# Ten products of a constant block first on TensorE, x in three loads, two first weight pieces of four tiles, and the first norm's squares behind all splits of x

## The chip, the cores and the metric

The kernel runs on one core of a Trainium2 chip. The metric is device time in microseconds (us). Work is spread over TensorE (PE for products, PEld for its weight loads), VectorE (DVE), ScalarE (ACT), GpSimd (POOL) and SyncE (SP, which only issues transfers here).

## The reference, cut to what matters

A two-layer hybrid block is followed by one layer of a second block, all on a sequence of 256 positions and a width of 1024. Of the first block, only its start bears on this change:

```python
def rmsnorm(x, g):
    y = x * rsqrt(mean(x * x, axis=-1, keepdims=True) + EPS)
    return y * g
def swiglu(x, wg, wu, wd):
    return (silu(x @ wg) * (x @ wu)) @ wd        # 1024 -> 2816 -> 1024
h = x
for i in range(2):
    h = h + 0.5 * swiglu(rmsnorm(h, ffn1_norm[i]), ffn1_wg[i], ffn1_wu[i], ffn1_wd[i])
    h = h + hybrid_mixer(rmsnorm(h, mix_norm[i]), ...)
    h = h + 0.5 * swiglu(rmsnorm(h, ffn2_norm[i]), ...)
    h = h + sigmoid(rmsnorm(h, ple_norm[i]) @ ple_w_gate[i]) * (p[i] @ ple_w_proj[i])
# then the second block: pooled and convolved branches, gates, a squared-ReLU feed-forward layer
```

## The kernel before

Everything is kept channels-first: x is eight blocks of 128 channels by 256 positions (`h`). The weights are 4948 tiles of 128x128 numbers, in the order in which they are used, and come as *pieces* of up to eight tiles. A piece lands in `raw` (or, for the first six, in `extra`, which is borrowed space); ACT rounds it to `whi`, DVE takes the rest `wlo = raw - whi`, and TensorE forms each product of a tile and a block of x as three: `hs` high with `whi`, `hs` low with `whi`, `hs` high with `wlo`, each 128x256. x is split in the same way: `split_scaled` makes the high part of a block on ACT and its low part on DVE, both in `hs`, scaled by the gain in `vec`.

The first layer's products do not wait for the norm: they take x scaled by the gain alone, and the norm's factor `row` is applied when a result leaves its bank (`gate` in `ffn`). The norm is a chain: the squares of the eight blocks (`square`: ACT squares into `sq`, DVE adds into `acc`), two column sums on TensorE (`side<-ones,acc`), a few small DVE steps, two products that spread the factor over the partitions (`side<-ident,small`), and a copy to `row` on ACT. There are seven banks for results. The first four units (`heads_of`) run side by side, block of x by block of x: each block meets four tiles. From tile 32 on (tiles are counted from 0 in TensorE's order) a unit of eight tiles has a bank of its own, and tile 56 needs the first bank again, so it waits for the first `gate`.

The order in which instructions stand on each engine is made by a small event simulation (`Flow`) in the kernel's own code, with planned costs; each engine then works its instructions strictly in that order. Piece boundaries (`PIECES`) are an input to it, so a change there renames buffers and moves single instructions throughout the program. Pieces are two and four tiles, then eight each; with the two first sizes 2 and 4 all later pieces begin at 6 plus a multiple of 8. ACT's DMA queue loads 32 columns of `vec` and x in four parts (one, one, two and four blocks), SP's queue the weights.

Of the kernel before, what the change touches and what calls it, by code (L numbers as in the profile page):

```python
# [17 lines left out]
P = 128  # L18
T = 256
D = 1024  # L20
ND = D // P
# [21 lines left out]
def piece_sizes():  # L43

    out, n = [], 0
    for size in (2, 4):
        out.append(size)
    n = sum(out)
    for stop in (*WHOLE, NTILES):
        while n < stop:  # L50
            out.append(min(S, stop - n))
            n += out[-1]
    return out


PIECES = piece_sizes()
FIRST = np.concatenate([[0], np.cumsum(PIECES)])

# [135 lines left out]
class Build:  # L194
# [91 lines left out]
    def feed(self):  # L286

        self.ready = [Event() for _ in PIECES]
        self.done = [Event() for _ in PIECES]
        self.at = [None] * len(PIECES)  # L290
        for q, cnt in enumerate(PIECES):
            raw = yield from self.raws.get()
            n, w = int(FIRST[q]), cnt * P
            self.nc.sync.dma_start(raw[:, :w], self.wall[n * P * P:(n * P + w) * P].rearrange("(p w) -> p w", p=P))
            if q < 4:
                a, b = self.xpieces[q]
                self.spawn(self.x_here(a, b), self.flow.use("dma", 0.365 * (b - a)) + 2.2)
            if q == 9:
                self.nc.sync.dma_start(self.vec[:, self.early:], self.vecd[:, self.early:])
            wait = self.flow.use("dma", w * P * 4 / 360e3) + 2.35  # L300
            self.spawn(self.piece(q, raw, w), wait)
# [189 lines left out]

    def setup(self):
        nc = self.nc
        self.early = a = 32
        self.xpieces = ((0, 1), (1, 2), (2, 4), (4, 8))
        nc.scalar.dma_start(self.vec[:, :a], self.vecd[:, :a])
        for b, c in self.xpieces:
            nc.scalar.dma_start(self.h[:, b:c, :], self.xT[:, b:c, :])
        self.xev = [Event() for _ in range(ND)]
        self.flow.use("dma", 1.8)  # L500
        make_identity(nc, self.ident)
        nc.vector.memset(self.ones, 1.0)
        nc.vector.memset(self.shim, 0.0)

        nc.vector.memset(self.mask, 0.0)
        nc.gpsimd.affine_select(out=self.mask, in_=self.mask, pattern=[[1, P]], compare_op=ALU.is_ge,
                                fill=NEG, base=0, channel_multiplier=-1)
        self.chains = 0
        self.started = [Event() for _ in PIECES]
        extra = self.big.tile([P, 6, S * P], F32, name="extra", tag="X")  # L510
        self.extra = [extra[:, i, :] for i in range(6)]
        more = self.big.tile([P, 8, 8], F32, name="more", tag="more")
        self.small[18:] = [more[:, i, :] for i in range(6)]
        self.raws.free[:0] = self.extra
        for cv in self.cv.free:
            nc.vector.memset(cv[:, :16], 0.0)
        self.act(self.small[0], self.ones[:, :8], AF.Silu)

    def first(self, op, s, gain):
        for n in range(ND):  # L520
            yield self.xev[n]
            yield from self.split_scaled(op, n, self.h[:, n, :], gain(n))
            self.spawn(self.square(s, self.h[:, n, :]))

    def x_here(self, a, b):
# [907 lines left out]
```

## Time and profile before

| | |
|---|---|
| median of three runs | 1811.37 us (1809.21 to 1815.61) |
| profiled execution, its own time | 1810.08 us |
| its span in the profile | 1808.3 us |
| TensorE busy | 1778.2 us (98%) |
| VectorE busy | 1320.9 us (73%) |
| ScalarE busy | 1050.3 us (58%) |
| mean granted TensorE clock | 0.996 |

The span is the time from the first to the last instruction that the profiler recorded; 1.8 us lie around it. A row of groups gives busy time, the mean duration of one, and the idle time before the group with what ended it. A row of a timeline begins with its start and its length in microseconds, merged over equal instructions. The chain lists, in order of time, the work that the end of the program can be followed back to.

### The profile page before, as it was taken

Reading aid. Unit: us, or ns where it says so; the run is one execution under the profiler, and the core shown is the slowest. Engines: PE = TensorE matmul, PEld = TensorE weight load, DVE = VectorE, ACT = ScalarE, POOL = GpSimd, SP = SyncE. Lnnn points to the kernel's source line nnn. Section 1 sums busy time; section 2 is a strip of 40 time slices with the busy share of each in tenths; the row PEclk is TensorE's granted clock in tenths of the full one; section 3 lists DMA queues with packets and bytes.
Section 4 is the critical chain, followed back from the end, with each engine's and each line's share of the span. In section 5 each row is a group of like instructions: output and inputs, shape, how many; then the busy total and the mean of one; then the engine's idle time right before and its main releaser. Section 6 shows DMA issues by size and latency. Waiting matters only on the chain.

```text
span 1808.3 us, 36543 instructions
## 1 busy us (share of the span) xinstructions
PE 1778.2 (98%) x14904; PEld 1737.8 (96%) x14904; DVE 1320.9 (73%) x2243; ACT 1050.3 (58%) x1711; POOL 10.5 (1%) x22
## 2 busy tenths in 40 slices
PE   8999999999999999999999999999999999989997
PEld 8999999999999999999999999999999999889985
DVE  7666789888676666866678988767666689877643
ACT  6454668665455544654456866555554478656542
POOL 0000000000000000000000000000000000000000
PEclk9999999999999999999999999999999999999998
DMA  7666576665766666566667656576666653546652
GB/s 248 198 192 195 163 258 191 207 192 157 206 185 199 194 195 185 189 195 196 192 175 248 195 198 192 159 206 193 202 194 194 196 176 121 184 142 210 192 193 76
DMA packets 92552, 342.78 MB, mean 190 GB/s; under 512 B 10432, under 2 KB 10944, under 8 KB 91360
## 3 DMA queue, kind: packets, MB, share of 16 engines
q1 hardware_dynamic: 89856, 325.13, 59.3%
q0 software_dynamic: 1520, 13.73, 2.1%
q8 instruction: 116, 1.90, 0.4%
q10 hardware_dynamic: 1008, 1.59, 0.2%
q14 instruction: 52, 0.43, 0.1%
HBM read 339.26 MB, written 1.15 MB: 188 GB/s over the span
## 4 chain that ended last, share of the span: by engine, by line
PE 91%; DVE 4%; DMA 2%; ACT 2%; issue 1%; ACTq 0%; DVEq 0%; SPq 0%
PE bank L237 90%; DVE wlo L244 1%; DMA raw<-in_w 1%; PE side L237 1%; DVE cv L257 1%; ACT whi L266 0%; ACT L266 0%; PE bank L722 0%; DMA h<-in_x 0%; DVE small L257 0%; DVE hs L257 0%; DVE dec L244 0%; DVE acc L244 0%; DVE t L244 0%; DVE vv L244 0%
## 5 line engine op out<-in xcount | busy, mean ns | idle before, releaser
L237 PE MATMUL bank<-hs,whi 128*128 128x256 f32 x6928 | 1206.1, 279 | 11.7 <-ACT whi L266 7.3
L237 PEld LDWEIGHTS bank<-hs,whi 128*128 128x128 f32 x6928 | 1049.9, 189 | 18.8 <-ACT whi L266 7.6
L244 DVE TENSOR_TENSOR wlo<-raw,whi 128x1024 fp32r<-128x1024 f32 (+1 forms) x602 | 733.0, 1220 | 373.3 <-ACT whi L266 370.3
L266 ACT ACTIVATE whi<-raw 128x1024 fp32r<-128x1024 f32 (+1 forms) x602 | 635.5, 1058 | 634.3 <-issue 320.5
L237 PE MATMUL bank<-hs,wlo 128*128 128x256 f32 x3464 | 961.9, 278 | 1.9 <-DVE wlo L244 1.9
L237 PEld LDWEIGHTS bank<-hs,wlo 128*128 128x128 f32 x3464 | 653.6, 189 | 2.9 <-DVE wlo L244 2.9
L237 PE MATMUL bank<-V,whi 128*128 128x256 f32 x1920 | 326.7, 276 | 0.0
L237 PEld LDWEIGHTS bank<-V,whi 128*128 128x128 f32 x1920 | 288.8, 188 | 0.0
L237 PE MATMUL bank<-V,wlo 128*128 128x256 f32 x960 | 265.0, 276 | 0.0
L237 PEld LDWEIGHTS bank<-V,wlo 128*128 128x128 f32 x960 | 180.2, 188 | 0.0
L237 PE MATMUL bank<-whi,V 128*128 128x512 f32 x256 | 80.0, 392 | 0.0
L244 DVE TENSOR_TENSOR t<-bank,row 128x256 f32<-128x256 f32 x159 | 64.5, 416 | 14.6 <-PE bank L237 10.3
L257 DVE SCALAR_TENSOR_TENSOR cv<-bank,vec,cv 128x253 f32<-128x253 f32 (+2 forms) x144 | 63.3, 472 | 1.7 <-ACT cv L266 1.3
L244 DVE TENSOR_TENSOR vv<-bank,t 128x256 f32<-128x256 f32 x152 | 62.5, 418 | 1.9 <-ACT t L266 1.6
L244 DVE TENSOR_TENSOR V<-vv,V 128x256 fp32r<-128x256 f32 x152 | 62.2, 419 | 1.6 <-ACT V L266 1.2
L266 ACT ACTIVATE V<-vv 128x256 fp32r<-128x256 f32 x152 | 59.9, 403 | 2.1 <-DVE vv L257 1.6
L237 PEld LDWEIGHTS bank<-whi,V 128*128 128x128 f32 x256 | 48.1, 188 | 10.1
L244 DVE TENSOR_TENSOR acc<-acc,sq 128x256 f32<-128x256 f32 x108 | 45.4, 420 | 8.5 <-ACT sq L266 7.9
L237 PE MATMUL bank<-wlo,V 128*128 128x512 f32 x128 | 50.2, 392 | 0.0
L266 ACT ACT_TABLE_LOAD x37 | 47.5, 1283 | 3.7 <-issue 3.1
L266 ACT ACTIVATE dec<-dec,tb 128x256 f32<-128x256 f32 (+1 forms) x128 | 49.5, 444 | 0.1
L237 PE MATMUL bank<-x,raw 128*128 128x256 f32 x208 | 45.2, 379 | 0.0
(149 smaller groups left out, 1108.0 us busy)
## 6 DMA issues: line engine op xcount, KB each, us to landing
raw<-in_w SPq DMA_DIRECT2D x613, 512.0 KB, 4.2
dec<-cum_d POOLq DMA_DIRECT2D x8, 1536.0 KB, 10.0
extra<-in_w SPq DMA_DIRECT2D x4, 512.0 KB, 8.0
h<-in_x ACTq DMA_DIRECT2D x1, 512.0 KB, 8.3
praw<-in_p POOLq DMA_DIRECT2D x2, 256.0 KB, 3.7
gain<-in_row POOLq DMA_DIRECT2D x1, 512.0 KB, 4.2
out<-o SPq DMA_DIRECT2D x2, 256.0 KB, 2.5
out<-o ACTq DMA_DIRECT2D x2, 256.0 KB, 2.5
```

Source lines behind the costliest of these rows:

```text
L237: self.nc.tensor.matmul(ps, w, x, start=start, stop=stop, **k)
L244: self.nc.vector.tensor_tensor(out, a, b, op=op)
L257: self.nc.vector.scalar_tensor_tensor(out, a, s, b, op0=op0, op1=op1)
L266: self.nc.scalar.activation(out=out, in_=a, func=func, **k)
```

## The change

Four edits, all at the start of the program. (1) Ten products of the constant block `ones` with itself (128x128, f32, into the `side` bank) stand first on TensorE; nothing reads their result. (2) x comes in three parts (two, two and four blocks), and the first 32 columns of `vec` come through SP's queue, behind the first weight piece. (3) The first two pieces hold four tiles each, so that all later pieces begin at a multiple of 8; the piece of two tiles that stood ahead of the stretch of whole tiles (`WHOLE`) is gone, and there is one piece fewer. (4) In the first norm, the squares are started after all eight splits instead of one after each.

```diff
-    for size in (2, 4):
+    for size in (4, 4):
...
             self.nc.sync.dma_start(raw[:, :w], self.wall[n * P * P:(n * P + w) * P].rearrange("(p w) -> p w", p=P))
-            if q < 4:
+            if q == 0:
+                self.nc.sync.dma_start(self.vec[:, :self.early], self.vecd[:, :self.early])
+            if q < len(self.xpieces):
...
-        self.early = a = 32
-        self.xpieces = ((0, 1), (1, 2), (2, 4), (4, 8))
-        nc.scalar.dma_start(self.vec[:, :a], self.vecd[:, :a])
+        self.early = 32
+        self.xpieces = ((0, 2), (2, 4), (4, 8))
         for b, c in self.xpieces:
             nc.scalar.dma_start(self.h[:, b:c, :], self.xT[:, b:c, :])
...
+        for _ in range(10):
+            self.mm(self.side.free[0][:, :P], self.ones, self.ones, cost=0.4)
...
         for n in range(ND):
             yield self.xev[n]
             yield from self.split_scaled(op, n, self.h[:, n, :], gain(n))
+        for n in range(ND):
             self.spawn(self.square(s, self.h[:, n, :]))
```

What stands on ACT from the first split of x on. Before (`hs<-h,vec` is the split of a block of x, `whi<-extra` that of a weight piece, `sq` and `acc` are squares):

```order
L266 ACTIVATE hs_94<-h,vec 128x256
L266 ACTIVATE whi_78<-extra 128x256
L266 ACTIVATE hs_94<-h,vec 128x256
L266 ACTIVATE acc_111<-h 128x256
L266 ACTIVATE whi_80<-extra 128x512
L266 ACTIVATE sq_109<-h 128x256
L266 ACTIVATE hs_94<-h,vec 128x256
L266 ACTIVATE whi_82<-extra 128x1024
```

The third weight piece (`whi_82`) stands behind the split of the third block of x.

On ACT at the same place now:

```order
L266 ACTIVATE hs_94<-h,vec 128x256
L266 ACTIVATE whi_78<-extra 128x512
L266 ACTIVATE hs_94<-h,vec 128x256
L266 ACTIVATE whi_80<-extra 128x512
L266 ACTIVATE hs_94<-h,vec 128x256 x3
L266 ACTIVATE whi_82<-extra 128x1024
L266 ACTIVATE hs_94<-h,vec 128x256
L266 ACTIVATE whi_84<-extra 128x1024
```

The squares are gone from here, and the third weight piece stands behind the split of the fifth block, which comes with the last part of x.

On TensorE before, the column sums of the first norm stood in the first unit that has a bank of its own (`bank_70`), behind 34 tiles:

```order
L237 MATMUL bank_69<-hs_94,wlo_79 128x256
L237 MATMUL bank_70<-hs_94,whi_78 128x256 x2
L237 MATMUL bank_70<-hs_94,wlo_79 128x256
L237 MATMUL bank_70<-hs_94,whi_78 128x256 x2
L237 MATMUL bank_70<-hs_94,wlo_79 128x256
L237 MATMUL side<-ones,acc_111 128x128 x2
```

They stand in the midst of that unit, two of its tiles ahead of them. On TensorE now, they stand in the unit after it (`bank_71`), behind 45 tiles:

```order
L237 MATMUL bank_71<-hs_94,whi_80 128x256 x2
L237 MATMUL bank_71<-hs_94,wlo_81 128x256
L237 MATMUL bank_71<-hs_94,whi_80 128x256 x2
L237 MATMUL bank_71<-hs_94,wlo_81 128x256
L237 MATMUL side<-ones,acc_111 128x128 x2
```

They moved back by eleven tiles. The two products that spread the factor (`side<-ident,small`) moved likewise from behind 43 tiles to behind 55, one tile ahead of tile 56.

## The prediction

> **What bounds the kernel now.** I read the page first, then TensorE's waits, then the chain and the timelines of the first 31 us, where the change lies. The page:
>
> ```profile
> span 1808.3 us, 36543 instructions
> PE 1778.2 (98%) x14904; PEld 1737.8 (96%) x14904; DVE 1320.9 (73%) x2243; ACT 1050.3 (58%) x1711; POOL 10.5 (1%) x22
> ...
> PE 91%; DVE 4%; DMA 2%; ACT 2%; issue 1%; ACTq 0%; DVEq 0%; SPq 0%
> ```
>
> TensorE has work in 98% of the span, so only an idle or slow TensorE is time to win. Its waits (total, times, longest) and its pace in a long quiet window (length, PE busy with the number of products, clock, DMA share, GB/s):
>
> ```profile
> PE bank L237 <- ACT whi L266: 7.3, 2, 6.1
> ...
> 30.00:240.00 210.00, 210.00 (x1855) 1.00 0.66 194
> ```
>
> The largest wait, 7.3 us, is for the first weights, at the start. Elsewhere a product takes 210/1855 = 0.113 us, a tile of three 0.34. The chain and TensorE's timeline at the start:
>
> ```profile
> 1.66 6.04 DMA h<-in_x
> 7.72 0.51 ACT hs L266
> ...
> 8.54 0.53 ACT whi L266
> ...
> 9.11 13.64 PE bank L237 x96
> 22.75 0.44 PE side L237 x4
> ```
>
> ```profile
> 6.13 0.80 PE L237 MATMUL bank<-hs,whi 128*128 128x256 f32 x2 [6.13 <-ACT whi L266]
> ...
> 9.11 0.80 PE L237 MATMUL bank<-hs,whi 128*128 128x256 f32 x2 [1.20 <-ACT whi L266]
> ...
> 13.42 0.63 PE L237 MATMUL bank<-hs,whi 128*128 128x256 f32 x2
> ...
> 14.05 0.41 PE L237 MATMUL bank<-hs,whi 128*128 128x256 f32 x2
> ...
> 31.09 0.39 PE L237 MATMUL bank<-hs,whi 128*128 128x256 f32 x2
> ```
>
> Tile 0 starts at 6.13, tile 2 at 9.11, after a wait for the second block of x. From 9.11 TensorE does not stop, but until 14.05 a tile takes 0.63, afterwards 0.34: half rate for 4.94 us of unbroken work, then full rate. Tile 9 starts at 14.05, tile 56 at 31.09. Had tile 0 begun at full rate at 6.13 and never stopped, tile 9 would start at 9.19, so the start holds at most 4.9 us. That is 0.27% of the time; 0.3% (5.4 us) is about what a measurement of this kernel can tell from no change.
>
> **The loads.** Issue rows (SP's first six merged, SP's third and fifth, ACT's last), and issue to landing for single transfers, read in windows that hold one issue of each queue:
>
> ```profile
> 0.74 4.78 SPq L294 DMA_DIRECT2D extra<-in_w  x6
> ...
> 1.65 0.42 SPq L294 DMA_DIRECT2D extra<-in_w  x1
> ...
> 3.46 0.58 SPq L294 DMA_DIRECT2D extra<-in_w  x1
> ...
> 2.62 0.45 ACTq L498 DMA_DIRECT2D h<-in_x  x1
> ```
>
> ```profile
> extra<-in_w SPq DMA_DIRECT2D x1, 256.0 KB, 3.8
> h<-in_x ACTq DMA_DIRECT2D x1, 128.0 KB, 4.0
> ...
> extra<-in_w SPq DMA_DIRECT2D x1, 512.0 KB, 5.9
> ...
> h<-in_x ACTq DMA_DIRECT2D x1, 512.0 KB, 8.3
> ...
> extra<-in_w SPq DMA_DIRECT2D x1, 512.0 KB, 8.5
> ```
>
> The last part of x (512 KB) was issued at 2.62 and landed at 10.9. Now it is ACT's third transfer, not its fifth, and issued near 1.7. Upper bound: issued before it were 1424 KB, now 1040 KB; the 384 KB less, at the 416 GB/s of the window 9.11:14.05 (below), are 0.95 us, so 9.96. Lower bound: the third weight piece (512 KB) landed at 1.65 + 5.9 = 7.55 when it was the last of 1040 KB issued; the last part of x is now the last of 1552 KB: 7.55 + 1.26 = 8.8; rows of x twice as long may hasten the early transfers, which I allow 0.8 for, so 8.0. I take **9.0**, nearest the weight row, because both are early in the same two queues. The first part of x and the first weights, 256 KB each, land by 0.74 + 3.8 to 4.0, about 4.7. That `vec` goes by SP costs one issue (0.45 us) on SP's queue ahead of the second piece, which is wanted only after tile 3.
>
> **ACT, DVE and TensorE after it.** The durations, from the timelines of ACT, then DVE, then PE:
>
> ```profile
> 8.44 0.61 ACT L266 ACTIVATE whi<-extra 128x512 fp32r<-128x512 f32 x1
> ...
> 9.27 0.49 ACT L266 ACTIVATE hs<-h,vec 128x256 fp32r<-128x256 f32 x1
> 9.67 1.04 ACT L266 ACTIVATE whi<-extra 128x1024 fp32r<-128x1024 f32 x1
> ```
>
> ```profile
> 0.84 0.17 DVE L502 MEMSET ones<- 128x128 f32 x1 [0.84 <-PEq L1428]
> ...
> 13.34 1.22 DVE L244 TENSOR_TENSOR wlo<-extra,whi 128x1024 fp32r<-128x1024 f32 x1
> 14.48 0.48 DVE L257 SCALAR_TENSOR_TENSOR hs<-h,vec,hs 128x256 fp32r<-128x256 f32 x1
> 14.88 0.42 DVE L244 TENSOR_TENSOR acc<-acc,sq 128x256 f32<-128x256 f32 x1
> 15.21 1.22 DVE L244 TENSOR_TENSOR wlo<-extra,whi 128x1024 fp32r<-128x1024 f32 x1
> ...
> 23.23 0.16 DVE L262 TENSOR_SCALAR small<-side 128x2 f32<-128x2 f32 x1 [0.46 <-PE side L237]
> ...
> 27.28 0.42 DVE L244 TENSOR_TENSOR t<-bank,row 128x256 f32<-128x256 f32 x1 [1.87 <-ACT row L266]
> ```
>
> ```profile
> 26.21 0.61 PE L237 MATMUL side<-ident,small 128*128 128x128 f32 x4
> ```
>
> From start to start a wide `wlo` takes 1.14 us, a low split of x 0.40, an addition 0.33.
>
> *Tiles 0 to 7.* First split at 4.7, first weights 0.40 later, 0.61 long: tile 0 at 5.75 instead of 6.13. Both first pieces feed all four banks, so eight tiles follow without x's last part.
>
> *The ten products.* Two of this shape cost 0.44 us at full rate (the row `side` at 22.75), so 0.44 each at half rate: 4.4 us from 1.1, when `ones` is set, to 5.5. They lie in idle time; with 0.25 us of cover, and if the cover were gone the wait below would hide it. They begin unbroken work at 1.1, so by the 4.94 us above full rate is there near 6.0. At full rate tiles 0 to 7 are over by about 9.3 (bounded by the second piece's splits); at half rate they would end at 11.1, and tile 9 would start 0.6 later than worked out next.
>
> *Tile 8: what is late next.* On ACT the third piece now stands behind the split of block 4, which waits for x's last part at 9.0, and everything behind it waits too. Weights: 9.0 + 0.40 + 1.04 = 10.44. `wlo` on DVE: to 11.7. Tile 8's third product follows, tile 9 starts at **11.8**, 2.25 us sooner than 14.05. After that ACT and DVE keep ahead: two splits and a piece for eight tiles are 0.8 + 1.14 = 1.94 us on DVE, TensorE needs 2.72.
>
> *The squares.* Taken from between the splits they free ACT and DVE there, and then come late. From `wlo` of the third piece at 10.5 DVE does nine wide `wlo`, three low splits and seven additions: 10.26 + 1.20 + 2.31, to 24.3. TensorE reaches the column sums behind 45 tiles at 11.8 + 36 x 0.34 = 24.0, to 24.5. The small steps took 26.21 - 23.23 = 2.98, so the spreading products are ready to run at 27.5; TensorE reaches them at 11.8 + 46 x 0.34 + 0.44 = 27.9. From their start to the first `t` were 1.07 and its length 0.42: the bank is free at 29.4. TensorE, done with the spreading (0.44) and one tile (0.34) at 28.7, waits 0.7. Before, `t` ended at 27.7, far ahead of tile 56. So tile 56 starts at 29.4 instead of 31.09: **1.7 us** remain. With 8.0 for the landing it is 2.7, with 9.96 it is 0.7, with 10.7 nothing.
>
> *New boundaries, one piece fewer.* One `whi` and one `wlo` of 602 go, on engines with idle time; TensorE's tiles are the same. I put it at nothing, bounded by the places below where DVE and ACT are full:
>
> ```profile
> 9.11:14.05 4.94, 4.94 (x21) 4.72 (x22) 4.71 (x9) 4.94 (x11) 0.00 (x0) 1.00 1.03 416
> 1610.42:1616.69 6.27, 2.00 (x9) 1.33 (x9) 3.99 (x18) 1.30 (x3) 0.00 (x0) 0.86 0.28 91
> 280.00:300.00 20.00, 19.44 (x169) 19.19 (x168) 18.97 (x32) 19.94 (x38) 0.00 (x0) 1.00 0.53 171
> 1010.00:1030.00 20.00, 19.22 (x168) 19.02 (x168) 19.05 (x31) 19.95 (x38) 0.00 (x0) 1.00 0.56 169
> ```
>
> (Length, then PE, PEld, DVE, ACT, POOL busy, clock, DMA share, GB/s. The clock column reads 1.00 in the first window although products took twice their time there; I go by durations.)
>
> **The sum**: 1810.08 - 1.7 = 1808.4 for an execution like the profiled one. That one lies 1.3 under the median of the three runs, so I say 1811.37 - 1.7 = **1809.7**.
>
> A rule on the clock: the Trainium skill, page "TensorE: Matmul & The Clock Gate", Part 1, says that TensorE starts at half rate and is released after a window of about 3.4 us of activity, a window that runs freely. The trace agrees: 4.94 us of unbroken work. By that rule, an estimate, the release now falls between 4.5 and 7.9 us; the sum stays, because tile 9 waits for `wlo` either way. The same page reckons the ramp at under 1% of a usual span, which speaks against a large gain here.
>
> **Rivals.**
> 1. *Paid in full.* All of x lands early enough that tile 8 hardly waits. Then DVE's work up to the norm's small steps sets tile 56: the fifth piece was issued at 3.46 and landed 8.5 later, at 12.0; with 1.04 for its `whi` and 0.1 to pass it on, from its `wlo` at 13.2 seven pieces, two splits and seven additions take 11.1, to 24.3, and 2.98 + 1.07 + 0.42 less the last `wlo` (1.14, if the small steps pass it) make 27.6: gain 3.5, time 1807.9. For it: x's share of the early bytes grows. Against: 8.8 from the weight row.
> 2. *Slower: the rate falls back in the new gap.* From 9.3 TensorE idles until 10.4, does two products, and idles until 11.7. Near 1610.42:1616.69 it was busy 2.00 of 6.27 us and the mean clock fell to 0.86. If the same happens here, 4.94 us at half rate follow, 7.7 tiles x 0.29 = 2.3 us: 31.7 at tile 56, 0.6 later than before, 1812.0. It decides from a gap as long as that one (some 6 us with little work); this one is 2.4. By the clock page's rule an idle window of 3.4 us is needed, and the gap stays under it.
> 3. *Nothing.* x's last part lands at 10.7 or later, as it did before (10.9): 1811.4.
> 4. *The later stalls move.* In the two mixers TensorE idled 0.56 us (280:300) and 0.78 us (1010:1030) for full ACT and DVE; with other boundaries both may go (with the 1.7, 1808.4) or double (1811.0).
>
> **Chances.** My forecast 0.55; rivals in order 0.13, 0.10, 0.08, 0.14. The forecast's own range is 1808.7 to 1810.7; the rivals span 1807.9 to 1812.0. The three runs of before spread over 6.4 us, so medians add about 2 at either end: 1805.8 to 1813.5. No case reaches 0.3% in itself; with the spread, under 1805.9 gets 0.11, over 1816.8 0.04, between them 0.85.
>
> **What would show it.** In the profile of the changed kernel: ten products on `side` from 1.1 to 5.5; tile 0 near 5.7; products of 0.11 from about 6 on; ACT waiting for `h<-in_x` at its fifth split, until 9.0; a TensorE wait for `wlo` of the third piece near 11.7; a wait of about 0.7 us ahead of tile 56 near 29. I am wrong if the last part of x lands outside 8 to 10, if tile 9 runs at half rate, or if a stall behind 280 us grows by more than the start gains.

## The result: 0.6% slower, and the profile after

The changed kernel took **1820.35 us** (median of 16 runs, 1815.02 to 1829.71), the kernel before 1809.14 us beside it (16 runs, 1806.3 to 1815.71). The ratio is 1.0063, with a 95% interval of 1.0049 to 1.0077: about 11 us lost, where 1.7 were to be gained. The profiled execution of the changed kernel took 1825.71 us itself, so it lies in the upper part of its runs.

The page of the changed kernel (span; busy time and number of instructions; chain by engine):

```profile
span 1823.9 us, 36518 instructions
...
PE 1792.0 (98%) x14924; PEld 1750.7 (96%) x14924; DVE 1325.3 (73%) x2242; ACT 1049.2 (58%) x1708; POOL 10.5 (1%) x22
...
PE 93%; DVE 2%; ACT 2%; DMA 2%; issue 1%; DVEq 0%; SPq 0%; ACTq 0%
```

The first thing to see is TensorE's busy time: 1792.0 us, 13.8 more than before, for the same tiles and twenty more instructions (each of the ten products shows as two). Those twenty are some 4 us, all at the start. So most of the loss does not look like waiting at all: TensorE is *busy longer* with the same work. The second is in its waits (total, times, longest; before, then changed):

```profile
PE bank L237 <- DVE wlo L244: 1.9, 4, 0.8
...
PE bank L237 <- DVE vv L244: 1.1, 2, 0.6
```

```profile
PE bank L237 <- DVE wlo L244: 6.0, 6, 2.2
PE bank L237 <- DVE vv L244: 2.5, 2, 1.2
...
PE bank L237 <- ACT whi L266: 1.7, 1, 1.7
```

The wait for the first weights fell from 7.3 us to 1.7, though some 4 us of that wait now hold the ten products. In return the waits for `wlo` rose from 1.9 to 6.0 (one of them is 2.2 long), and those for `vv` from 1.1 to 2.5.

To see where, I set the two traces side by side by tile, from the start of the third product of one tile to that of another:

| tiles | before | changed | difference |
|---|---|---|---|
| start to tile 57 | 31.67 | 31.26 | -0.4 |
| 57 to 540, first feed-forward layer | 164.22 | 170.66 | +6.4 |
| 740 to 850, first mixer | 40.59 | 42.88 | +2.3 |
| 1000 to 1200, first mixer | 81.37 | 82.13 | +0.8 |
| 1984 to 2030 | 17.02 | 17.63 | +0.6 |
| 2780 to 2860, second mixer | 30.50 | 33.62 | +3.1 |
| 3020 to 3200, second mixer | 74.41 | 74.95 | +0.5 |
| 4010 to 4060 | 18.84 | 19.53 | +0.7 |
| 4330 to 4450 | 54.32 | 52.67 | -1.7 |
| 4450 to 4690 | 81.60 | 84.80 | +3.2 |

All other stages together make +0.1. Two kinds of loss stand out. One lies in long stretches in which TensorE never waits: +6.4 and +3.2. A quiet window of each (before, then changed: length, PE busy with the number of products, weight loads, DVE, ACT, clock, DMA share, GB/s; products into `bank` alone):

```profile
40.00:190.00 150.00, 150.00 (x1326) 150.00 (x1326) 17.47 (x42) 0.00 (x0) 1.00 0.68 196
```

```profile
40.00:190.00 150.00, 150.00 (x1276) 150.00 (x1275) 17.16 (x42) 0.00 (x0) 1.00 0.57 188
```

TensorE is busy without a break in both, at a granted clock of 1.00, and yet does 1326 products in one and 1276 in the other: 0.113 and 0.118 us each, **0.340 or 0.353 us for a tile of three**. This is 4% and has nothing to do with the half rate at the start.

The other kind is new waits in the mixers. Around the longest one, at tile 2792 (changed kernel; ACT, then DVE, then PE):

```profile
1001.38 1.06 ACT L266 ACTIVATE whi<-raw 128x1024 fp32r<-128x1024 f32 x1 [1.78 <-DMA raw<-in_w]
...
1006.34 1.06 ACT L266 ACTIVATE whi<-raw 128x1024 fp32r<-128x1024 f32 x1 [3.60 <-DMA raw<-in_w]
1007.31 0.55 ACT L266 ACTIVATE cv<-bank,vec 128x256 f32<-128x256 f32 x1
```

```profile
1003.77 0.47 DVE L257 SCALAR_TENSOR_TENSOR cv<-bank,vec,cv 128x254 f32<-128x254 f32 x1
1007.89 0.48 DVE L257 SCALAR_TENSOR_TENSOR cv<-bank,vec,cv 128x255 f32<-128x255 f32 x1 [3.65 <-ACT cv L266]
1008.29 1.22 DVE L244 TENSOR_TENSOR wlo<-raw,whi 128x1024 fp32r<-128x1024 f32 x1
```

```profile
1006.99 0.39 PE L237 MATMUL bank<-hs,whi 128*128 128x256 f32 x2
1009.56 0.38 PE L237 MATMUL bank<-hs,wlo 128*128 128x256 f32 x1 [2.18 <-DVE wlo L244]
```

Read from the top: ACT stood 3.60 us for a weight piece that landed late, while the large loads `dec<-cum_d` were under way. TensorE did not need that piece yet: it began tile 2792 with its own `whi` at 1006.99, before the late piece's `whi` was done (1007.40), and it came to the late piece only at 1012.25. The `whi` of tile 2792 is the row at 1001.38, done at 1002.44. But on DVE a step of the convolution (`cv`) stood ahead of this tile's `wlo`, and that step waited 3.65 us for ACT's `cv`, which stood behind the late piece's `whi`. So `wlo`, whose input had been there since 1002.44, began at 1008.29, some 4 us after DVE had become free, and TensorE waited 2.18. In the kernel before, ACT waited for a late piece in the same mixer too, but DVE's row held that piece's own `wlo` next, and TensorE did not wait there:

```profile
988.54 1.23 DVE L244 TENSOR_TENSOR wlo<-raw,whi 128x1024 fp32r<-128x1024 f32 x1 [3.41 <-ACT whi L266]
```

The start itself (PE and ACT, changed kernel):

```profile
1.06 4.27 PE L237 MATMUL side<-ones 128*128 128x128 f32 x20 [1.06 <-DVE ones L503]
6.98 0.50 PE L237 MATMUL bank<-hs,whi 128*128 128x256 f32 x2 [1.66 <-ACT whi L266]
...
8.17 0.37 PE L237 MATMUL bank<-hs,wlo 128*128 128x256 f32 x1
8.33 0.63 PE L237 MATMUL bank<-hs,whi 128*128 128x256 f32 x2
...
11.54 0.45 PE L237 MATMUL bank<-hs,whi 128*128 128x256 f32 x2
...
12.67 0.28 PE L237 MATMUL bank<-hs,wlo 128*128 128x256 f32 x1
...
30.56 0.50 PE L237 MATMUL bank<-hs,whi 128*128 128x256 f32 x2 [0.58 <-DVE t L244]
```

```profile
5.91 0.51 ACT L266 ACTIVATE hs<-h,vec 128x256 fp32r<-128x256 f32 x1 [2.25 <-DMA vec<-in_vec]
...
8.07 0.63 ACT L266 ACTIVATE whi<-extra 128x512 fp32r<-128x512 f32 x1 [0.74 <-DMA extra<-in_w]
8.61 1.29 ACT L266 ACTIVATE hs<-h,vec 128x256 fp32r<-128x256 f32 x3
```

The same stretch by the granted clock (length, PE busy with the number of products, clock, DMA share, GB/s):

```profile
4.80:8.21 3.41, 1.53 (x11) 1.00 1.00 387
8.21:11.63 3.42, 3.42 (x19) 0.50 1.03 419
```

Tile 0 begins at 6.98, later than before (6.13), because the first split waited for `vec`. It begins at full rate, falls to half rate at 8.2 and is back at full rate near 11.6. Tile 9 (third product) comes at 12.67 instead of 14.30, and of these 1.6 us most is given back: 0.9 around the wait ahead of tile 56 that the late squares bring (0.58 by itself), 0.35 by the slower pace ahead of it.

### The profile page after: what moved, and what is told of

The parts are those of the page before. It is cut to its first block, busy times and chain, and to the rows that moved or that the text cites. A ratio compares the mean times of both kernels' runs of the same rounds, so it can differ in the third digit from the quotient of the medians.

```text
span 1823.9 us, 36518 instructions
## 1 busy us (share of the span) xinstructions
PE 1792.0 (98%) x14924; PEld 1750.7 (96%) x14924; DVE 1325.3 (73%) x2242; ACT 1049.2 (58%) x1708; POOL 10.5 (1%) x22
## 4 chain that ended last, share of the span: by engine, by line
PE 93%; DVE 2%; ACT 2%; DMA 2%; issue 1%; DVEq 0%; SPq 0%; ACTq 0%
PE bank L237 91%; DMA raw<-in_w 1%; PE side L237 1%; DVE wlo L244 1%; DVE cv L257 1%; ACT dec L266 1%; ACT L266 1%; ACT whi L266 0%; PE bank L727 0%; DVE small L257 0%; DMA vec<-in_vec 0%; ACT cv L266 0%; DVE t L244 0%; DVE o L257 0%; ACT xb L266 0%
## 5 line engine op out<-in xcount | busy, mean ns | idle before, releaser
L257 DVE SCALAR_TENSOR_TENSOR cv<-bank,vec,cv 128x255 f32<-128x255 f32 (+2 forms) x144 | 64.0, 472 | 10.5 <-ACT cv L266 10.2
L266 ACT ACTIVATE cv<-bank,vec 128x256 f32<-128x256 f32 x48 | 26.9, 560 | 32.6 <-PE bank L237 32.5
```

Source lines behind the costliest of these rows:

```text
L257: self.nc.vector.scalar_tensor_tensor(out, a, s, b, op0=op0, op1=op1)
L266: self.nc.scalar.activation(out=out, in_=a, func=func, **k)
```

## The experiments

The theory after the comparison (A): the loss is made by the new piece boundaries, through another order in the mixers; the start is worth little; and which of the two paces TensorE has in a long stretch is a second, separate cause. Rivals: the start causes the loss (the ten products, the loads or the late squares), or the pace explains all of it. The order of instructions shows that the pieces alone set the order from tile 530 on. The groups of runs below come from the times of single runs, the stage times from one profiled execution each.

**Boundaries alone.** The kernel before with one number changed:

```diff
-    for size in (2, 4):
+    for size in (4, 4):
```

> Only the first two pieces are 4 and 4 tiles; the loads, the squares and the missing ten products are as before. Built, its order of instructions from tile 530 on is that of the changed kernel, on all engines. Theory A (the new piece boundaries reorder ACT and DVE in the mixers and behind the second feed-forward layers, and that makes the stalls there longer): against the kernel before, tile 850 comes some 2 us later by stalls between tiles 740 and 850, tile 2850 some 3 us later by those between 2780 and 2850, in all +6 to +8 us besides what the pace of TensorE does. Theory B (the slow pace of 0.353 us a tile from tile 57 to 540 in the changed kernel comes from the ten products or the new start): here that stretch runs at 0.340, and the total is +6 to +8. Theory C (the pace is drawn anew in each execution): that stretch is slow in some executions and not in others, and single times split into two groups some 6.5 us apart.

Measured: 1819.12 us (7 runs, 1815.75 to 1825.81), ratio **1.0046** (1.0024 to 1.0069). In its profile the mixers are those of the changed kernel (43.03, 82.13, 33.53 and 74.95 us in the four mixer rows of the table), and tiles 57 to 540 take 164.22, as before. So one digit costs 0.46%.

**All but the boundaries.** The changed kernel with the old pieces:

```diff
-    for size in (4, 4):
+    for size in (2, 4):
```

> The changed kernel with the old first pieces of 2 and 4 tiles; ten products, loads and squares as changed. From tile 530 on its order is that of the kernel before. Theory A: the later stalls are those of before, so 0 to -2 us against the kernel before, from the start alone. Theory B: the slow pace from tile 57 to 540 stays, +4.5 to +6.5 us. Theory C: single times in two groups, the median within 2 us of before.

Measured: 1809.89 us (12 runs), ratio 1.0005 (0.9989 to 1.0022). The mixers are those of before (41.65, 81.37, 28.79, 74.41). So the other three edits neither gain nor lose what can be measured: 0.46 and 0.05% make 0.51 of the 0.63%, and the intervals leave room for the rest. Its times fall into two groups, seven from 1807.6 to 1810.1 and five from 1814.1 to 1819.5; the profiled run (1819.45) had the slower pace in both long stretches (170.66 and 84.8 us).

**Both kernels profiled again**, with no edit:

> The changed kernel once more, for the pace of TensorE in its stretches. Theory B (set by the program): 0.353 us a tile again from tile 57 to 540 and behind the second block's norm (tiles 4450 to 4690). Theory C (drawn in each execution): at least one of the long stretches differs from the first profile. The stalls between tiles 740 and 850, and 2780 and 2850, are as in the first profile in either case, if A holds.

> The kernel before once more, for the pace. Theory B: 0.340 again from tile 57 to 540 and from 4450 to 4690, and 0.353 from 4350 to 4420. Theory C: at least one of its stretches differs from the first profile.

Measured: the changed kernel 1822.22 us, with 170.66 us again for tiles 57 to 540, but 81.6 us for 4450 to 4690: the same program, another pace in that stretch. The mixers were as slow as the first time (42.09, 82.13, 34.27, 74.95). Before: 1812.1 us, 164.22 and 81.6 us, but 44.74 us for tiles 740 to 850, where the first profile had 40.59. So the mixer's extra time repeats in the stages 1000 to 1200, 2780 to 2860 and 3020 to 3200; in 740 to 850 a single profile tells little.

**The parts of the start.** The ten products alone, added to the kernel before; and the loads with the late squares, without the ten products (both with the old pieces, edits as in the diff of the change).

> The kernel before plus the ten products of ones and nothing else; loads, pieces and squares as before. Theory A (the boundaries cost about 7 us, the start is worth about 1 us): within 2 us of before, median 1808 to 1812, and tile 9 not more than 1 us earlier than the 14.30 and 13.65 us of the two profiles of before, since the second block of x still lands near 7.7. Theory B (the ten products put TensorE into its slower pace, 0.353 us a tile of three products, between tiles 57 and 540): the time falls into two groups 6.5 us apart, or the profile shows 170.7 us for tiles 57 to 540 instead of 164.2; median up to 1816.

> The kernel before with the three loads of x, vec behind the first weights, and the squares behind the splits; pieces 2 and 4, and no ten products. Theory A: 1808 to 1811, as with the ten products (1809.9); the order from tile 530 on is that of before, so tiles 2780 to 2860 take 28.8 to 30.5 us as there. Theory B (the ten products cause the slow stretch of tiles 57 to 540): no execution in the upper group, and a median 2 us lower than with them, near 1808. If instead the loads or the late squares bring it, the upper group is there as well.

Measured: ten products alone 1811.8 us, ratio 1.0013 (0.9997 to 1.0028); loads and squares 1810.27, ratio 1.001 (0.9995 to 1.0025). Neither gains. The ten products are not what brings the slower pace: without them four of twelve runs still lie above 1813.5 us (with them alone, four of twelve). The profiled run with the ten products had 0.353 us between tiles 57 and 540, the one without had 0.340.

**The boundaries mended.** The changed kernel with a third number, so that all pieces from tile 14 on begin where they did before:

```diff
-    for size in (4, 4):
+    for size in (4, 4, 6):
```

> The changed kernel with one more number: pieces of 4, 4 and 6 tiles, then eight each, so that from tile 14 on all pieces begin where they began before (6 plus a multiple of 8), with as many pieces as before. All four edits of the start stay. Theory A (the cost lies in where the later pieces begin, from tile 530 on): the seven us come back whole, 1808 to 1811; tiles 2780 to 2860 take 28.8 to 30.5 us, not 33.5 to 34.3; tile 9 stays at 12.6 to 13.0. Rival (the cost comes from the two pieces of four at the start, or from the start itself): 1816 to 1820.

Measured: 1811.71 us (12 runs), ratio 1.0011 (0.9997 to 1.0026); tiles 2780 to 2860 in 30.05 us, tile 9 at 12.03. With the two pieces of four still at the start, the mixers' loss is gone: theory A holds, the rival that blames the first pieces falls. A second profile of it,

> A second look at the changed kernel with pieces of 4, 4 and 6 (all four edits of the start, and the boundaries of before from tile 14 on), for the pace alone: tiles 57 to 540 at 164.2 or 170.7 us, the rest as in the first look: tile 9 near 12.0, tiles 2780 to 2860 at 30 us.

gave 1809.31 us, 164.22 us for tiles 57 to 540, tile 9 at 11.77. In both profiles tile 9 was some 2 us earlier than before, and a wait ahead of tile 56 took it back: tiles 55 to 57 took 3.21 and 3.17 us instead of 0.68. With these pieces the column sums stand behind 51 tiles (45 in the changed kernel), so TensorE waits 0.6 us ahead of the spreading products as well, and 0.93 ahead of tile 56.

**Another offset.** Three pieces of four, so that later pieces begin at 4 plus a multiple of 8:

```diff
-    for size in (4, 4):
+    for size in (4, 4, 4):
```

> The changed kernel with first pieces of 4, 4 and 4, so that later pieces begin at 4 plus a multiple of 8, an offset that neither kernel has. Theory F (any other offset lets the plan write another order through the mixers, and stalls come with it): slower than before like the changed kernel, 1813 to 1822, with other stages at fault. Theory G (only the offset 0 is unlucky, or the missing piece ahead of the whole tiles costs): 1808 to 1812.

Measured: 1824.14 us (4 runs), ratio 1.0077 (1.0057 to 1.0097), and other stages at fault: 40.61 us for tiles 4330 to 4430 (37.45 before, 36.24 in the changed kernel), 19.04 for 1984 to 2030 (17.02, 17.63), 20.89 for 4010 to 4060 (18.84, 19.53). The second mixer's 2780 to 2860 took 32.90, as slow as with the changed kernel's pieces (32.5 to 34.3). So it isn't one unlucky number: of three offsets tried, the one that the kernel came with is the best by 0.5 to 0.8%.

**What makes the mixer wait: late weights or the order?** In both kernels half of each load `dec<-cum_d` is left out; GpSimd fills the other heads with a constant, so the order on the other engines stays and the results of the mixers are not those of the reference:

```diff
-            nc.gpsimd.dma_start(dec, cd[g * 8:(g + 1) * 8, :].partition_broadcast(P))
+            nc.gpsimd.dma_start(dec[:, 0:4], cd[g * 8:g * 8 + 4, :].partition_broadcast(P))
+            nc.gpsimd.memset(dec[:, 4:8], NEG)
```

> The kernel before with the second half of the heads of each dec block filled with a constant by GpSimd, where the loads dec<-cum_d brought it: it leaves out half of these loads, 0.79 MB of 1.57 MB each, in both mixers; instructions on the other engines keep their order. To be set against the same edit in the changed kernel, stage by stage. Tiles 2780 to 2860 took 28.8 to 30.5 us with the old boundaries: 27.5 to 29 expected under both theories, tiles 740 to 850 39.5 to 41.

> The changed kernel with the second half of the heads of each dec block filled with a constant by GpSimd instead of loaded: it leaves out half of these loads; the order on the other engines stays that of the changed kernel. Tiles 2780 to 2860 took 33.5 to 34.3 us with the new boundaries, with ScalarE waiting 3.60 us for a weight piece beside the loads of dec, and TensorE then 2.18 and 1.46 us. Theory C (the new order puts a weight piece's split behind work that waits for weights held up by these loads): with half the loads at least 2.5 us of the 4 come back, tiles 2780 to 2860 take 29 to 31 us. Theory D (the order alone: the split stands behind other work on VectorE and ScalarE, however soon the weights land): 33 or more. Tiles 1000 to 1200 (0.76 more than before) and 3020 to 3200 (0.54 more), which lie behind these loads, stay as they are under both.

Measured: tiles 2780 to 2860 in 28.79 us (before) and 30.15 us (changed): with the whole loads ten profiles with the later pieces where they were before had 28.8 to 30.5 there, five with the new ones 32.5 to 34.3 (means 29.5 and 33.3). So the two are 1.4 us apart instead of 3.8, with one profile each. Waits in that mixer, in the changed kernel, and with half the loads:

```profile
ACT whi L266 <- DMA raw<-in_w: 5.4, 2, 3.6
DVE cv L257 <- ACT cv L266: 5.0, 3, 3.6
...
PE bank L237 <- DVE wlo L244: 3.6, 2, 2.2
```

```profile
...
ACT whi L266 <- DMA raw<-in_w: 1.8, 1, 1.8
DVE cv L257 <- ACT cv L266: 1.7, 1, 1.7
...
PE bank L237 <- DVE wlo L244: 1.1, 1, 1.1
```

The three fall together: ACT's wait for weights, DVE's wait behind it, TensorE's wait at the end. The wait of 2.18 at tile 2792 is gone; the 1.1 that is left is the one at tile 2832 (1.46 in the changed kernel). So some 2.4 of these 3.8 us need both the late transfer and the order that passes it on. The 0.76 us in tiles 1000 to 1200 and 0.54 in 3020 to 3200 stayed to the hundredth: these loads have no part in them.

**What sets the pace.** Extra f32 products (`ones` times `ones`, into `side`, read by nobody) in the stretch of tiles 57 to 540, placed outside the plan so that nothing else moves; the number of them at each place is told in the expectations. The first of these runs also had ordinary products (a tile's `whi` with a block of x) between tiles 1250 and 1900; thirteen stood there, not the nine expected.

```diff
         self.order.append(key)
+        if n in range(90, 540, 50):
+            for _ in range(2):
+                self.nc.tensor.matmul(self.side.free[0][:, :P], self.ones, self.ones, start=True, stop=True)
```

> The kernel before with extra products whose results nobody reads: nine pairs of ones times ones (128x128, f32, on side), one pair each 50 tiles from tile 90 to 490, and nine single products of the ordinary kind (a weight tile's high part and a block's high part, 128x256) between tiles 1250 and 1900. They stand outside the plan, so all other instructions keep their order. Theory (the pace of 0.340 or 0.353 us a tile is set anew by f32 products on side and held between them): the pace changes at one or more of the nine pairs in one execution, and only there. Rival 1 (any extra product can change it): it changes at the ordinary ones too. Rival 2 (it is a state of the chip in time, or follows where transfers stand): it changes at neither, or elsewhere. Time: 9 x 0.44 + 9 x 0.11 = 5 us over before, plus 0.67 us for each stretch of 50 tiles at the slower pace.

Measured: 1814.91 us, and the pace stayed at 0.340 through all nine pairs, and through the thirteen ordinary products. But at the second norm's own pairs (`ones,acc` behind tile 550, then `ident,small`) it went to 0.353 and back to 0.340. Neither theory as written. The next two vary the number.

> The changed kernel with extra f32 products ones times ones on side, whose results nobody reads, at nine places of the stretch of tiles 57 to 540: two at tile 90, one at 140, one at 190, two at 240, two into different halves of the bank at 290 and at 340, three at 390, two at 440 and at 490. In both profiles of the changed kernel this stretch ran at 0.353 us a tile throughout. Theory (the pace is a phase that f32 products shift, and 0.340 keeps itself once it is there): it begins at 0.353 behind tile 56 and goes over to 0.340 at one of the first places, and stays there, so tiles 57 to 540 take 164.2 plus 17 products x 0.22 = 3.7, so 168 to 169 us. Rival (these products leave the pace as it is, as the nine pairs left 0.340 as it was in the kernel before; only a stall or the norm's own products set it): 0.353 from tile 57 to 540, 170.7 + 3.7 = 174.4 us.

> The kernel before with extra f32 products of the same kind: two into different halves of the side bank at tiles 90, 140 and 290, one at 190 and 240, three at 340 and 390, four at 440, two into one half at 490. Nine pairs into one half left the pace at 0.340 in this kernel. If the number of products or the half of the bank sets the phase, the pace changes at single places of these; if only a stall or the norm's own products do, tiles 57 to 540 stay at 0.340 and take 164.2 + 22 x 0.22 = 169.0 us.

Measured: places with **one or three** products changed the pace at once and for the whole 50 tiles up to the next place, seven times of seven, in either direction. Places with **two or four** left 0.340 as it was, ten times of ten beside the nine above, whichever half of the bank they wrote; the one place where two met 0.353 (tile 440 of the changed kernel) turned it to 0.340. One case is little. The column sums of the first two norms are two products as well, and over all eighteen profiles they took 0.340 to 0.353 each time (24 of 24), but 0.353 to 0.340 only 5 times of 12. Timeline of TensorE in the changed kernel at a single product (start and length):

```profile
58.59 0.28 PE L237 MATMUL bank<-hs,wlo 128*128 128x256 f32 x1
...
58.93 0.28 PE L237 MATMUL bank<-hs,wlo 128*128 128x256 f32 x1
...
59.39 0.38 PE L345 MATMUL side<-ones 128*128 128x128 f32 x2
...
60.20 0.28 PE L237 MATMUL bank<-hs,wlo 128*128 128x256 f32 x1
...
60.55 0.28 PE L237 MATMUL bank<-hs,wlo 128*128 128x256 f32 x1
```

Third products of successive tiles lie 0.34 apart ahead of it and 0.35 behind it. So the pace behaves like a phase that TensorE's stream holds until something disturbs it; what it is inside the engine no run shows. A stall sets it too: in five profiles of the changed kernel's start (its own two, that with half loads, and two with added products), tiles 57 and after ran at 0.353 twice and at 0.340 three times, all behind the same wait ahead of tile 56. Two of them (the second profile of the changed kernel, and half loads) ran alike up to that wait, with 82 products from 15 to 24 us in both, and differed behind it: 1353 and 1405 products from 31 to 190 us. The total of the first of these two probes (1823.7 us) tells nothing about the fix, since its stretch began at 0.340 by itself.

**Two pairs behind tile 56**, in the changed kernel, to turn the pace in every execution:

```diff
+        for half in {60: (0, 0), 64: (0, 0)}.get(n, ()):
+            self.nc.tensor.matmul(self.side.free[0][:, half * P:(half + 1) * P], self.ones, self.ones, start=True, stop=True)
```

> The changed kernel with two pairs of f32 products (ones times ones, on side, nobody reads them) at tiles 60 and 64, outside the plan. A pair cost 0.47 us elsewhere, so 0.94 us. Theory E (a pair turns 0.353 into 0.340 and leaves 0.340 as it is, so tiles 57 to 540 run at 0.340 in every execution): the upper group of the changed kernel, near 1826, goes; the profile shows 0.340 from tile 64 on, and tiles 57 to 540 take 165.2 us; median 1816 to 1819, from 1820.35. Rival (what a pair does to 0.353 is as often nothing): both groups stay, median 1820 to 1822.

Measured: 1818.2 us (five runs, 1817.3 to 1822.54), ratio 1.0048 (1.0032 to 1.0063); tiles 57 to 540 took 165.15 us. No run near 1826, as expected, but the interval overlaps that of the changed kernel (1.0049 to 1.0077), and the profiled run was at 0.340 already when it met the pairs. So it agrees with the theory and does not prove it.

**The best of the parts together**: loads, ten products, pieces of 4, 4 and 6, the squares where they were before, and the two pairs:

> The three loads of x, vec behind the first weights, the ten products and pieces of 4, 4 and 6 tiles; the squares stay where they were before the change (each behind its split), and two pairs of f32 products stand at tiles 60 and 64. The column sums are behind 34 tiles again, so no stall ahead of tile 56 is expected: tile 57 at 12.0 + 7.8 + 8.9 + 0.7 = 29.4 us, where before had 31.0 to 31.7 and the same start with late squares 31.9. Theory E and the mended boundaries together: 1809.4 - 1.9 + 0.9 = 1808.4, no upper group; faster than before by 0 to 2 us. If the squares hold DVE back by as much as they spare: 1809 to 1810. If the pairs do nothing to the pace: some executions near 1815.

Measured: 1810.41 us (11 runs, 1807.63 to 1813.56), ratio 1.0001 (0.9991 to 1.0011). No upper group and no wait ahead of tile 56, but no gain either: tile 9 came at 12.84, since with the squares back DVE was late with the third piece (0.49 us of wait at 12.38). No version beats the kernel before.

## Why the prediction was wrong, point by point

*New boundaries at nothing: this step failed, and it made the loss.* The prediction counted what the edit removes (one `whi`, one `wlo`) and not what the planner does with another input. (There were 608 of each before, not 602.) It gave the two known waits 1.3 us either way; the profiles with the new pieces, after subtracting the slower pace where they had it, are some 5 us longer than those with the old ones (1814.0, 1814.0 and 1814.3 us of span against 1808.3 and 1810.3), and the ratio of the boundaries alone, 1.0046, puts it at 8 us with an interval of 4 to 12. Rival 4 named the mechanism ("the later stalls move"), but with a price taken from two places that stall before. Those two did about double, as it said (0.56 to 1.47 at tile 792, 0.78 to 1.46 at tile 2832). What it lacked is the new wait of 2.18 at tile 2792 (0.28 before, at tile 2798) and the two waits for `vv` ahead of tiles 2006 and 4046, which went from 0.56 to 1.23 and 1.24: together some 3.2 us. The prediction's own sign of being wrong, a stall behind 280 us that grows by more than the start gains, is what came.

*A constant 0.34 us a tile: this step failed too.* The quiet window 30:240 showed one pace of two. At 0.353, 483 tiles cost 6.4 us, more than the whole start could bring. How often the stretch is slow: of runs with the old boundaries, 11 of 79 of the kernel before lie above 1813.5 us, and 18 of 48 of the four kernels with a changed start (all but the boundaries, ten alone, loads and squares, mended). That bound is my choice, and other stages vary as well (740 to 850 by some 5 us between profiles), so it is a hint that a new start lands on the slower pace more often, at a cost near 0.24 x 6.4 = 1.5 us on average; the profiles (none of six with the old loads and no ten products, four of twelve with either) point the same way.

*Tile 0 at 5.75: missed, 6.98.* The first split was put at 4.7, by the landing of x. It waited for `vec`, which had moved behind the first weight piece on SP's queue and let ACT start only at 5.91. The prediction priced that move as 0.45 us for the piece behind it and forgot the instruction that needs `vec`.

*The ten products: right in this execution, in part by luck, and undone.* They ran from 1.06 to 5.33 in idle time, and tile 0 began at full rate. But 1.66 us of idle time followed, and from 8.21 to 11.63 the granted clock was 0.50. This is rival 2, one gap earlier and after a shorter gap than it asked for. In the eleven profiles with the ten products it went three ways: full rate came between 4.6 and 5.7 us and held in two (5.39 in the first profile of the mended kernel, after an idle 1.05 us), came and fell back for 3.41 us in five, and came only between 9.97 and 13.42 us, long after tile 0, in four. The Trainium skill, page "TensorE: Matmul & The Clock Gate", Part 1, has a window of about 3.4 us that runs freely; the 3.41 us of half rate here agree with one such window, and so does it that other executions fell differently. The idle window of 3.4 us that rival 2 took from this page of the Trainium skill was not needed: TensorE was busy for 1.53 of the 3.41 us ahead of the fall.

*Tile 8 and tile 9 (11.8): nearly.* Tile 9 began at 12.44 (its third product is at 12.67). x's last part landed at 9.1, where 9.0 was taken, but the late second piece (0.74 us of ACT's wait at 8.07) had already moved the row.

*The squares: right in size.* A wait of 0.7 us ahead of tile 56 was worked out; 0.58 was measured. *The gain of 1.7 at tile 56* came out as 0.5 (30.56 instead of 31.09; 30.16 and 30.43 in the second profiles), since tile 9 gained 0.6 less than planned and the slower pace took part of the rest.

*The range.* It was built from places that wait in the profile of before, so it could hold neither a stage that gets a new wait nor a stretch that runs at another pace.

## What to carry to other kernels

Where an event simulation or planner writes the order, a change of its inputs (a piece size) is a new program everywhere behind it: compare the order in every stage, and price the edit by what other inputs of the same kind did, not by the instructions it removes. Where a wait is new, look for work that is ready but stands behind another piece's late load. Keep a start-up edit from leaking into the rest: one more number (4, 4, 6 instead of 4, 4) put back the mixers that it had shifted. And when TensorE's busy time grows with the same products, compare products per window ahead of any wait.

## What the hardware showed that was not expected

- At a granted clock of 1.00, without a wait, the same stream of products has two paces, 0.340 and 0.353 us for a tile of three (1326 or 1276 products in 150 us). A stall sets it; one or three 128x128 f32 products change it (seven of seven), two or four leave 0.340 as it is (nineteen of nineteen). Thirteen single ordinary products left it too. The column sums of the first two norms are two products as well, and yet they changed 0.340 to 0.353 each time (24 of 24). Why they differ from the inserted pairs stays open.
- Half rate can return for 3.41 us after an idle time of only 1.66 us, although 4.3 us of work preceded it and 1.2 us of work at full rate followed. The same ten products gave full rate at tile 0 in seven of eleven profiles, and full rate that held in two.
